# The Fourier part of a hybrid block on sums and differences of tokens and channels

## The chip, the cores and the metric

The kernel runs on one core of one Trainium2 chip. The metric is the device time in microseconds of one execution, and of several the median. A core has a matmul engine (PE, with its weight loads listed as PEld), a vector engine (DVE), a scalar engine (ACT), a general engine (POOL, also called GpSimd) and a queue engine (SP), each of which works through its own list of instructions in order and waits at semaphores for the others. Sixteen DMA engines move data between the chip's main memory and the core's on-chip memory.

## The reference, cut to what matters

One layer over 512 latent tokens (and 256 context tokens, which only feed the attention states): normalisation with modulation, one input projection of width 4128, two kinds of mixing, an output projection with a gated residual, and then experts.

```python
p = modulate(rms_norm(x, norm1_g), shift1, scale1) @ w_in
q, k, v, g, z_f, z_b, u = split(p)        # u: 1024 columns, the Fourier part
# attention heads (GLA): 4 heads over q, k, v and the gates from z_f, z_b
# Fourier part: 8 groups of 128 channels
uf = u.reshape(512, 8, 128)
y = jnp.fft.fft2(uf, axes=(tokens, channels), norm='ortho').real
mixed = concatenate([y_gla, y.reshape(512, 1024)], -1) @ w_out
x = x + gate1 * mixed
h = modulate(rms_norm(x, norm2_g), shift2, scale2)
aff = softmax(h @ w_router)               # 16 experts
gate, idx = top_k(aff.T, 64)              # each expert takes 64 tokens
# SwiGLU experts on the taken tokens, gated, scattered back; a final norm
```

The six modulation vectors come from silu(c) @ w_ada. The real part of a two-dimensional transform of real numbers is cos·cos − sin·sin over tokens l and channels c. The cosine is the same at l and 512 − l, and the sine changes its sign there; for the channels the same holds at c and 128 − c. Tokens 0 and 256 and channels 0 and 64 have no partner.

## The kernel before

**Products in three passes.** Matmul operands of the large products are split in two parts, a rounded one (hi) and the rest (lo), and a product is three matmuls: hi·hi, hi·lo and lo·hi (L481 to L483 for the input products, L875 to L877 for the output). Each has a stationary operand of 128 x 128, which is a tile of 128 tokens, and a moving one of 128 x 512 weights.

**The weights.** `Stream` (L155) brings `w_in` and `w_out` in chunks of 512 KB (two k rows of 128 by 512 columns). `load` issues a chunk's DMA on ACT's queue (L168), at most two chunks ahead; `split` makes hi with an ACT copy (L175) and lo with a DVE subtraction (L176), and chunks are split two ahead of the products that take them.

**The stages.** The stages run one after the other on PE: K, V and Q products (V and Q by `tokens`, L472), the gates G in two column blocks, the Fourier input u in two column blocks, and the output products in four blocks of 512 columns (L862 to L895) with 16 k rows each, the first 8 from the attention heads, the last 8 from the Fourier part. Then come the routing (L903 to L953, with the top-64 by eight rounds of MAX8 and MATCH_REPLACE8 at L935 and L936) and the experts. The Fourier stage reads tokens by stride (`four`) and folds them in its `ev` into halves with two DVE operations per tile.

**Work in the background.** `bg` is a planner: generators put their instructions between the products, and each `yield` says after how many microseconds of estimated PE time the next step stands (`bg.tick`). So the order of the program is set by estimates, and every engine then runs its list in that order. In the background run: the later modulation vectors (`ada_rest`, L416, 16 steps of one load of 1 MB on SP and one DVE operation at L430, the delay of a step is `RD[0]` or `RD[1]`), the attention heads (`gla_head`, L537) with the transposes of their gated output (`gla`, L678), the Fourier transforms (`fourier`, L698), and the routing logits of the output (`logits`, L850). Two vectors, i = 2 and 4, run in V and Q (`rest1`), i = 3 and 5 in the output products (`rest_out`, L760).

**Space.** All large tiles are pages of 128 x 2048 from a pool of 24 (`PG`); the expert weights are loaded ahead into pages as these come free (`pump`, L829, on SP's queue). Eight PSUM banks hold results.

## Time and profile before

| what | value |
|---|---|
| time, median of 3 runs | 1827.98 us (1825.45 to 1828.62) |
| the profiled execution | 1827.28 us, its span 1825.2 us |
| PE busy | 1728.1 us, 95% of the span |
| DVE busy | 689.0 us, 38% |
| ACT busy | 336.8 us, 18% |
| POOL busy | 5.5 us, 11 instructions |
| moved by DMA | 571.79 MB, mean 313 GB/s |

The stretches of the span are: V and Q products 161.3 to 339.4 us, gates 339.4 to 405 and 405 to 472, Fourier input 472 to 613.4, output products 613.4 to 821.5 (the transforms of the second half of the channels lie in the first 32.6 us), routing 821.5 to 845.3, and experts after it. A fast matmul is listed with 0.39 us, because matmuls overlap; what one costs is the distance from one start to the next. A matmul in full 32-bit precision has two rows in the trace.

### The profile page before, as it was taken

The numbers are of one execution on the slowest core, as the hardware profiler recorded it, in microseconds if no ns is written. First come the engines' busy times: TensorE is split into PE (matmuls) and PEld (weight loads), VectorE is DVE, ScalarE is ACT, GpSimd is POOL, SyncE is SP. The second block draws the span as 40 slices with busy tenths as digits, with TensorE's granted clock in tenths as the row PEclk, the third lists the DMA queues.
The fourth block names the chain that finished last, engine by engine and source line by source line (L and its number), as shares of the span: only waits on it lengthen the run. The fifth ranks groups of instructions, "written<-read, shape, count | busy, mean of one in ns | idle before, by whom it ended". The sixth has DMA issues, their size and how long they took to land.

```text
span 1825.2 us, 21307 instructions
## 1 busy us (share of the span) xinstructions
PE 1728.1 (95%) x8992; PEld 1049.1 (57%) x8992; DVE 689.0 (38%) x1072; ACT 336.8 (18%) x564; POOL 5.5 (0%) x11
## 2 busy tenths in 40 slices
...
GB/s 375 391 230 180 261 211 340 84 70 81 58 81 178 287 263 275 292 174 331 379 300 319 419 419 419 419 420 419 420 419 419 420 419 419 420 419 410 415 419 254
DMA packets 89695, 571.79 MB, mean 313 GB/s; under 512 B 9840, under 2 KB 12312, under 8 KB 27136
## 3 DMA queue, kind: packets, MB, share of 16 engines
...
q14 instruction: 25, 0.20, 0.0%
HBM read 566.21 MB, written 4.19 MB: 313 GB/s over the span
## 4 chain that ended last, share of the span: by engine, by line
PE 77%; DMA 15%; DVE 4%; ACT 3%; issue 1%; DVEq 0%; ACTq 0%; SPq 0%
PE bank L1072 18%; PE bank L1131 10%; DMA pg<-in_w_e_gate 7%; PE bank L991 6%; PE bank L481 5%; PE bank L482 5%; PE bank L483 5%; DMA pg<-in_w_e_up 4%; PE bank L875 3%; DMA pg<-in_w_e_down 3%; PE bank L877 3%; PE bank L876 3%; PE bank L1034 3%; PE bank L331 2%; PE bank L332 2%; PE bank L333 2%
## 5 line engine op out<-in xcount | busy, mean ns | idle before, releaser
L1072 PE MATMUL bank<-pg,pg 128*64 128x512 f32 x1856 | 435.2, 597 | 25.7 <-DMA pg<-in_w_e_up 13.9
L1072 PEld LDWEIGHTS bank<-pg,pg 128*64 128x64 f32 x1856 | 139.1, 136 | 287.9 <-issue 219.4
L1131 PE MATMUL bank<-pg,tp 128*64 128x512 f32 (+1 forms) x1056 | 233.4, 584 | 11.3 <-ACT tp L1099 10.8
L481 PE MATMUL bank<-pg,pg 128*128 128x512 f32 x448 | 184.5, 412 | 1.5 <-ACT pg L175 1.4
L482 PE MATMUL bank<-pg,pg 128*128 128x512 f32 x448 | 175.5, 392 | 0.8 <-DVE pg L176 0.8
L483 PE MATMUL bank<-pg,pg 128*128 128x512 f32 x448 | 175.5, 392 | 0.0
L176 DVE TENSOR_TENSOR pg<-pg,pg 128x1024 fp32r<-128x1024 f32 x96 | 117.4, 1223 | 130.9 <-ACT pg L175 120.8
L1131 PEld LDWEIGHTS bank<-pg,tp 128*64 128x64 f32 x1056 | 74.7, 137 | 145.3 <-issue 123.2
L995 DVE TENSOR_SCALAR pg<-bank,a,b 128x128 f32<-128x128 f32 x116 | 41.4, 406 | 302.6 <-PE bank L991 302.6
L430 DVE SCALAR_TENSOR_TENSOR pg<-pg,scol,pg 128x2048 f32<-128x2048 f32 x60 | 140.9, 2348 | 27.0 <-DMA pg<-in_w_ada 26.8
L175 ACT ACTIVATE pg<-pg 128x1024 fp32r<-128x1024 f32 x96 | 101.7, 1059 | 204.7 <-DVE pg L430 61.7
L1037 DVE TENSOR_TENSOR pg<-pg,bank 128x512 f32<-128x512 f32 (+1 forms) x132 | 79.7, 666 | 152.5 <-PE bank L1034 152.5
L991 PEld LDWEIGHTS bank<-pg,pg 128*128 128x128 f32 x896 | 104.0, 192 | 32.1 <-issue 28.4
L991 PE MATMUL bank<-pg,pg 128*128 128x128 f32 x896 | 111.5, 280 | 0.0
L875 PE MATMUL bank<-pg,pg 128*128 128x512 f32 x256 | 105.1, 410 | 0.0
L877 PE MATMUL bank<-pg,pg 128*128 128x512 f32 x256 | 100.1, 391 | 0.0
L876 PE MATMUL bank<-pg,pg 128*128 128x512 f32 x256 | 100.0, 391 | 0.0
L481 PEld LDWEIGHTS bank<-pg,pg 128*128 128x128 f32 x448 | 85.3, 190 | 21.5 <-ACT pg L175 1.9
L482 PEld LDWEIGHTS bank<-pg,pg 128*128 128x128 f32 x448 | 85.3, 190 | 17.7 <-DVE pg L176 1.1
L483 PEld LDWEIGHTS bank<-pg,pg 128*128 128x128 f32 x448 | 85.0, 190 | 17.8
L1106 ACT ACTIVATE tp<-bank 128x512 f32<-128x512 f32 x16 | 9.4, 597 | 431.4 <-PE bank L1072 431.4
L331 PE MATMUL bank<-pg,pg 128*128 128x512 f32 x192 | 72.3, 377 | 0.8 <-ACT pg L321 0.8
(256 smaller groups left out, 1611.7 us busy)
## 6 DMA issues: line engine op xcount, KB each, us to landing
pg<-in_w_e_gate SPq DMA_DIRECT2D x128, 1024.0 KB, 19.9
pg<-in_w_e_up SPq DMA_DIRECT2D x128, 1024.0 KB, 19.9
...
```

What stands on the lines that cost most here:

```text
L176: dve.tensor_sub(p[:, 1024:].bitcast(F32R), src, p[:, :1024])
L331: pe.matmul(o, w[0], h[0], start=first, stop=False, skip_group_check=sgc)
L430: dve.scalar_tensor_tensor(acc, p, scol[:, k:k + 1], acc, op0=OP.mult, op1=OP.add)
L481: pe.matmul(bs[t], h[0], whi[:, kk, :], start=k == 0, stop=False)
L482: pe.matmul(bs[t], h[0], wlo[:, kk, :], start=False, stop=False)
L483: pe.matmul(bs[t], h[1], whi[:, kk, :], start=False, stop=k == 15)
L875: pe.matmul(bs[t], h[0], whi[:, kk, :], start=k == 0, stop=False)
L876: pe.matmul(bs[t], h[0], wlo[:, kk, :], start=False, stop=False)
L877: pe.matmul(bs[t], h[1], whi[:, kk, :], start=False, stop=k == 15)
L991: pe.matmul(b[:, j * 128:(j + 1) * 128], X[t][:, k * 128:(k + 1) * 128], ohr[:, t, :], start=t == 0, stop=t == 3)
L1072: pe.matmul(gu[2 * m + f][64 * j:64 * j + 64, :], xe(pr, k)[:, 64 * j:64 * j + 64], v3(ps[2 * m + j], 2)[:, k2, f * 512:f * 512 + 512], st ...
L1131: pe.matmul(b[64 * j:64 * j + 64, :h.stop - h.start], hidt[:, 4 * f + k, 64 * j:64 * j + 64], v3(ps[j], 4)[:, k, h], start=f == 0 and k == ...
```

## The change

**Input products of the Fourier part.** They run on folded operands. The normalised tokens `hl` are folded while the second gate block runs (`fold_h`): POOL adds hi and lo, DVE makes the sums l + (512 − l) and the differences, which are split into hi and lo again in place. The host lays the columns of `w_in` out so that channels c and 128 − c stand in the two halves of a chunk, and `Stream.fold` makes their sum (DVE) and difference (POOL) before the split. One pass over 16 chunks then does what two column blocks did: sums of tokens meet sums of channels, differences meet differences. Token 256 is a product of one row; channel 64 comes with the gates' small product (`w_z` widened by 8 columns).

**Transforms.** They run on halves: 257 tokens with cosines, 255 with sines, and 64 channels of two groups together. Channel 64 of all groups goes by 8-row products.

**Output products.** The last 4 chunks of each column block of `w_out` are folded in the same manner (16 chunks of 32). The part of the result that is even in the output token is accumulated in banks 0 and 1 and the odd part in banks 2 and 3. The gated output of the heads is folded as well after its transposes. Two tiles (t, t + 2) are then combined to their sum and difference. The order of the tokens within the kernel is 0 to 256 and 511 down to 257: `x` is loaded in that order and the host puts the output back. The top-64 works on scores put back to the order of the tokens.

**Modulation.** Vector 3 moves from `rest_out` into `rest1`, and `RD[0]` falls from 5.0 to 3.4.

```diff
-RD = (5.0, 4.6)
+RD = (3.4, 4.6)
...
-            if self.nl < len(self.chunks) and self.nl < self.ns + 2:
+            if self.nl < len(self.chunks) and self.nl < (max(self.ns, self.nf) if self.ns in self.folded else self.ns) + 2:
...
+        def fold(self, j):
+            if j in self.folded and self.nf <= j:
+                while self.nl <= j:
+                    self.load()
+                r, f = self.raw(j), self.fw[j % 2]
+                dve.tensor_add(f[:, :512], r[:, :512], r[:, 512:])
+                pool.tensor_sub(f[:, 512:], r[:, :512], r[:, 512:])
+                self.nf = j + 1
         def split(self):
+            n = self.ns
             self.load()
-            src = self.raw(self.ns)
+            self.fold(n)
+            if self.ahead and n + 1 in self.folded:
+                self.load()
+                self.fold(n + 1)
+                self.load()
+            src = self.fw[n % 2] if n in self.folded else self.raw(n)
             p = PG.get()
             act.activation(p[:, :1024].bitcast(F32R), src, AF.Copy)
             dve.tensor_sub(p[:, 1024:].bitcast(F32R), src, p[:, :1024])
...
-    rest1 = rest((2, RD[0]), (4, RD[0]))
+    rest1 = rest((2, RD[0]), (4, RD[0]), (3, RD[0]))
...
-            act.activation(yt(m, 0), b, AF.Copy, scale=gng[:, m:m + 1])
-            dve.scalar_tensor_tensor(yt(m, 1), b, gng[:, m:m + 1], yt(m, 0).bitcast(F32),
-                                     op0=OP.mult, op1=OP.subtract)
+            y, z = tmp(), tmp()
+            act.activation(y, b, AF.Copy, scale=gngh[:, m:m + 1])
             BK.put(b)
+            dve.tensor_add(z[:, 0:1], y[:, 0:1], y[:, 256:257])
+            dve.tensor_sub(z[:, 256:257], y[:, 256:257], y[:, 0:1])
+            dve.tensor_add(z[:, 1:256], y[:, 1:256], y[:, 511:256:-1])
+            dve.tensor_sub(z[:, 257:512], y[:, 511:256:-1], y[:, 1:256])
+            act.activation(yt(m, 0), z, AF.Copy)
+            dve.tensor_sub(yt(m, 1), z, yt(m, 0).bitcast(F32))
...
+        def tokens_dft(p):
+            ps = slice(128 * p, 128 * p + 128)
+            vf, b = vfs[p % 2], BK.get()
+            d = DY[:, 260 + p:261 + p]
+            for i, (st, tb) in enumerate(((uv[:, 0, ps], CT[:, 0, :]), (uv[:, 1, ps], CT[:, 1, :]), (uv[0:1, 2, ps], row))):
+                pe.matmul(b[:, 0:256], st, tb[:, 0:256], start=i == 0, stop=i == 2, skip_group_check=True)
+                pe.matmul(d, st, tb[:, 256:257], start=p == 0 and i == 0, stop=i == 2, skip_group_check=True)
+            for i in range(2):
+                pe.matmul(b[:, 256:512], uv[:, 2 + i, ps], ST[:, i, :], start=i == 0, stop=i == 1, skip_group_check=True)
+            (dve.tensor_copy if p % 2 else act.copy)(vf[:, 0:512], b)
+            dve.tensor_copy(vf[:, 512:513], d)
...
-        yield from rest((3, RD[1]))
+        bg.drain(rest1)
...
+    def fold_h():
+        FF.append(PG.get())
+        ws.fw = [FF[0][:, 1024:2048], FF[0][:, 0:1024]]
+        x, y = FF[0][:, 0:512], FF[0][:, 512:1024]
+        pool.memset(y[:, 256:257], 0.0)
+        for k in range(NK):
+            while kdone[0] <= k:
+                yield 1.3
+            hi, lo = hl(k, 0), hl(k, 1)
+            if k % 4 == 0:
+                for s in range(2):
+                    act.copy(h256[:, k:k + 4, s], v3(HL[k // 4][s], 4)[:, :, 256].bitcast(F32R))
+            pool.tensor_add(x[:, 0:512], hi.bitcast(F32), lo.bitcast(F32))
+            act.copy(y[:, 0:1], x[:, 0:1])
+            dve.tensor_add(y[:, 1:256], x[:, 1:256], x[:, 511:256:-1])
+            dve.tensor_sub(y[:, 257:512], x[:, 1:256], x[:, 511:256:-1])
+            act.activation(hi, y, AF.Copy)
+            dve.tensor_sub(lo, y, hi.bitcast(F32))
+            yield 2.2
...
-        tokens(48 + 8 * c, four, ev)
+    bg.drain(hfold)
+    ws.ahead = True
+    bs = [BK.get() for _ in range(4)]
+    for k in range(NK):
+        whi, wlo = ws.take(FW0 + k)
+        for t, f in enumerate(lat):
+            h = (f(k, 0), f(k, 1))
+            i = t // 2
+            pe.matmul(bs[t], h[0], whi[:, i, :], start=k == 0, stop=False, skip_group_check=True)
+            pe.matmul(bs[t], h[0], wlo[:, i, :], start=False, stop=False, skip_group_check=True)
+            pe.matmul(bs[t], h[1], whi[:, i, :], start=False, stop=k == 15, skip_group_check=True)
+            bg.tick(0.65)
+        for s, w in ((0, whi), (0, wlo), (1, whi)):
+            pe.matmul(bs[2][0:1, :], h256[:, k, s:s + 1], w[:, 0, :], start=False, stop=k == 15 and s == 1,
+                      skip_group_check=True)
+        bg.tick(0.5)
+        ws.done(FW0 + k)
...
-            for kk in range(2):
-                k = 2 * j + kk
-                h = [yt(k, s)[:, t * 128:(t + 1) * 128] for s in range(2)]
-                pe.matmul(bs[t], h[0], whi[:, kk, :], start=k == 0, stop=False)
-                pe.matmul(bs[t], h[0], wlo[:, kk, :], start=False, stop=False)
-                pe.matmul(bs[t], h[1], whi[:, kk, :], start=False, stop=k == 15)
-            bg.tick(1.3)
-            if j == 7:
-                s = tmp()
-                dve.tensor_mul(s, bs[t], g1[0][:, cs])
-                dve.tensor_add(X[t][:, cs], X[t][:, cs], s)
-                act.activation(s, X[t][:, cs], AF.Square, accum_out=ssx[:, t, c:c + 1])
-                bg.add(logits(c, t), LD[0])
+            i, ts = t // 2, slice(t * 128, (t + 1) * 128)
+            for k, q in ((2 * j, 0), (2 * j + 1, 1)) if j < 4 else ((4 + j, i),):
+                h = [yt(k, s)[:, ts] for s in range(2)]
+                pe.matmul(bs[t], h[0], whi[:, q, :], start=k == 0, stop=False, skip_group_check=True)
+                pe.matmul(bs[t], h[0], wlo[:, q, :], start=False, stop=False, skip_group_check=True)
+                pe.matmul(bs[t], h[1], whi[:, q, :], start=False, stop=k == 11 and t == 3, skip_group_check=True)
+            if t == 2 and j >= 4:
+                for s, w in ((0, whi), (0, wlo), (1, whi)):
+                    pe.matmul(bs[2][0:1, :], dT[:, j - 4, s:s + 1], w[:, 0, :], start=False, stop=False,
+                              skip_group_check=True)
+            if t < 3 and j == 7:
+                y = Y64[0][0:72, ts if t < 2 else slice(256, 257)].bitcast(F32R)
+                pe.matmul(bs[t][0:128 if t < 2 else 1, :], y, W64[0][0:72, cs].bitcast(F32R), start=False, stop=True,
+                          skip_group_check=True)
+            bg.tick(1.3 if j < 4 else 0.75)
+            if j == 7 and t >= 2:
+                t0 = t - 2
+                ps, qs = tmp(), tmp()
+                dve.tensor_mul(ps, bs[t0], g1[0][:, cs])
+                dve.tensor_mul(qs, bs[t], g1[0][:, cs])
+                for x, f in ((X[t0][:, cs], dve.tensor_sub), (X[t][:, cs], dve.tensor_add)):
+                    dve.tensor_add(x, x, ps)
+                    f(x, x, qs)
+                for r in (t0, t):
+                    act.activation(ps if r == t0 else qs, X[r][:, cs], AF.Square, accum_out=ssx[:, r, c:c + 1])
+                    bg.add(logits(c, r), LD[0])
...
+    dve.tensor_copy(aft[:, 0:257], b[:16, 0:257])
+    dve.tensor_copy(aft[:, 257:512], b[:16, 511:256:-1])
...
+    for v in (work, sl):
+        dve.tensor_copy(aft[:, 0:255], v[:, 511:256:-1])
+        dve.tensor_copy(v[:, 257:512], aft[:, 0:255])
```

How the program's order moves is shown for three places. In these rows `pg_76_1343` is a page by its numbers, then come the operands and the size.

DVE in the V products, of the kernel before: L430 is a step of the modulation vector, L176 the split of a weight chunk.

```order
L430 SCALAR_TENSOR_TENSOR pg_76_1343<-pg_86_1497,scol,pg_76_1343 128x2048
L176 TENSOR_TENSOR pg_88_1528<-pg_6_99,pg_88_1528 128x1024
L430 SCALAR_TENSOR_TENSOR pg_76_1343<-pg_87_1524,scol,pg_76_1343 128x2048
L176 TENSOR_TENSOR pg_90_1571<-pg_6_99,pg_90_1571 128x1024
L430 SCALAR_TENSOR_TENSOR pg_76_1343<-pg_89_1549,scol,pg_76_1343 128x2048
L430 SCALAR_TENSOR_TENSOR pg_76_1343<-pg_91_1580,scol,pg_76_1343 128x2048
L176 TENSOR_TENSOR pg_93_1617<-pg_6_99,pg_93_1617 128x1024
L430 SCALAR_TENSOR_TENSOR pg_76_1343<-pg_92_1607,scol,pg_76_1343 128x2048
```

One or two steps stand between two splits there. The same place of the changed kernel, where the step is L472 and the split L204:

```order
L204 TENSOR_TENSOR pg_84_1457<-pg_6_103,pg_84_1457 128x1024
L472 SCALAR_TENSOR_TENSOR pg_76_1353<-pg_83_1447,scol,pg_76_1353 128x2048
L472 SCALAR_TENSOR_TENSOR pg_76_1353<-pg_85_1472,scol,pg_76_1353 128x2048
L204 TENSOR_TENSOR pg_87_1503<-pg_6_103,pg_87_1503 128x1024
L472 SCALAR_TENSOR_TENSOR pg_76_1353<-pg_86_1487,scol,pg_76_1353 128x2048
L472 SCALAR_TENSOR_TENSOR pg_76_1353<-pg_88_1512,scol,pg_76_1353 128x2048
L472 SCALAR_TENSOR_TENSOR pg_76_1353<-pg_89_1527,scol,pg_76_1353 128x2048
L204 TENSOR_TENSOR pg_91_1552<-pg_6_103,pg_91_1552 128x1024
```

Between two splits it is now mostly two steps, up to three.

DVE in the second gate block, of the kernel before: the decays of an attention head (L551 to L589) and one split (L176).

```order
L551 SCALAR_TENSOR_TENSOR pg_159_3068<-bank_107_3086,pg_159_3068 128x512
L552 SCALAR_TENSOR_TENSOR pg_159_3068<-bank_108_3087,pg_159_3068 128x256
L554 SCALAR_TENSOR_TENSOR pg_159_3068<-pg_72_1249,pg_159_3068 128x768
L176 TENSOR_TENSOR pg_160_3110<-pg_6_99,pg_160_3110 128x1024
L572 TENSOR_TENSOR pg_158_3067<-pg_158_3067 128x512
L573 TENSOR_SCALAR pg_158_3067<-pg_158_3067 128x256
L585 TENSOR_TENSOR st<-st 128x4
L586 TENSOR_TENSOR pg_158_3067<-pg_158_3067,pg_119_2089 128x512
L587 TENSOR_TENSOR pg_158_3067<-pg_158_3067,pg_72_1249 128x256
```

There the head and the split have DVE to themselves. The same place of the changed kernel: L594 to L631 are the head's, L204 is the split, L884, L885 and L887 belong to the fold of the tokens, and `pg_168_2855` is its working page.

```order
L597 SCALAR_TENSOR_TENSOR pg_177_3197<-pg_72_1256,pg_177_3197 128x768
L884 TENSOR_TENSOR pg_168_2855<-pg_168_2855 128x255
L885 TENSOR_TENSOR pg_168_2855<-pg_168_2855 128x255
L887 TENSOR_TENSOR pg_50_814<-pg_168_2855,pg_49_813 128x512
L204 TENSOR_TENSOR pg_178_3253<-pg_6_103,pg_178_3253 128x1024
L615 TENSOR_TENSOR pg_176_3196<-pg_176_3196 128x512
L616 TENSOR_SCALAR pg_176_3196<-pg_176_3196 128x256
L628 TENSOR_TENSOR st<-st 128x4
L629 TENSOR_TENSOR pg_176_3196<-pg_176_3196,pg_129_2144 128x512
L630 TENSOR_TENSOR pg_176_3196<-pg_176_3196,pg_72_1256 128x256
L631 TENSOR_TENSOR pg_176_3196<-pg_176_3196,pg_71_1255 128x512
```

A chunk's sum, difference and low part are put between the head's operations, and all of them wait in one list.

ACT around the start of the Fourier input, of the kernel before, with what each waits for: L168 loads a chunk, L175 makes its high part.

```order
L460 COPY pg_184_3807<-bank_156_3862 128x512 [waits PE_49]
L168 DMA pg_6_99<-in_w_in 128x1024 [waits DVE_49]
L175 ACTIVATE pg_188_3873<-pg_6_99 128x1024 [waits DMAHW2_49]
L168 DMA pg_6_99<-in_w_in 128x1024 [waits DVE_49]
L175 ACTIVATE pg_192_3908<-pg_6_99 128x1024 [waits DMAHW3_49]
L717 COPY pg_190_3884<-bank_157_3919 128x512 [waits PE_49]
```

Each load waits for DVE alone and has its high part right behind it. The same of the changed kernel: L180 loads, L203 makes the high part of a folded chunk, L886 that of a folded token row block, L668 is a head's.

```order
L883 COPY pg_168_2855<-pg_168_2855 128x1 [waits DVE_49,Pool_49]
L886 ACTIVATE pg_63_1043<-pg_168_2855 128x512 [waits DVE_49,Activation_49]
L180 DMA pg_6_103<-in_w_in 128x1024 [waits DMAHW3_49]
L180 DMA pg_6_103<-in_w_in 128x1024 [waits DMAHW4_49,DVE_49,Pool_49]
L180 DMA pg_6_103<-in_w_in 128x1024 [waits DMAHW5_49,DVE_49,Pool_49]
L203 ACTIVATE pg_183_3454<-pg_168_2855 128x1024
L668 COPY pg_180_3263<-bank_120_3463 128x256 [waits PE_49]
L669 COPY pg_180_3263<-bank_120_3463 128x256
```

A load now waits for DVE and POOL, which fold the chunk in the buffer that it overwrites, and stands ahead of the next high part in ACT's list.

## Rows read from the trace of the kernel before

**Rows 1.** The page: span, engines (busy, share, instructions), chain that ended last by engine.

```profile
span 1825.2 us, 21307 instructions
...
PE 1728.1 (95%) x8992; PEld 1049.1 (57%) x8992; DVE 689.0 (38%) x1072; ACT 336.8 (18%) x564; POOL 5.5 (0%) x11
...
PE 77%; DMA 15%; DVE 4%; ACT 3%; issue 1%; DVEq 0%; ACTq 0%; SPq 0%
```

**Rows 2.** Busy time by stretch: us, PE, PEld, DVE, ACT, POOL, PEclk, DMA share, GB/s.

```profile
161.30:250.00 88.70, 88.70 (x391) 72.58 (x390) 53.81 (x34) 17.41 (x20) 0.00 (x0) 1.00 0.66 243
250.00:339.40 89.40, 89.40 (x402) 73.24 (x401) 53.60 (x33) 17.75 (x20) 0.95 (x1) 1.00 0.73 265
339.40:405.00 65.60, 63.20 (x345) 51.34 (x344) 29.14 (x44) 31.39 (x54) 0.95 (x1) 1.00 0.22 71
405.00:472.00 67.00, 61.37 (x350) 49.61 (x348) 42.86 (x72) 33.89 (x64) 0.95 (x1) 0.97 0.20 66
472.00:613.40 141.40, 136.36 (x699) 112.12 (x700) 85.56 (x124) 59.60 (x105) 0.95 (x1) 1.00 0.37 127
...
646.00:821.50 175.50, 175.38 (x891) 138.33 (x893) 99.77 (x86) 48.49 (x76) 0.00 (x0) 1.00 0.68 252
821.50:845.30 23.80, 16.58 (x73) 8.16 (x70) 17.15 (x41) 2.55 (x7) 0.00 (x0) 0.86 1.00 415
850.00:1000.00 150.00, 148.65 (x816) 73.84 (x814) 37.69 (x104) 9.56 (x15) 0.00 (x0) 1.00 0.83 324
1000.00:1750.00 750.00, 718.88 (x3512) 314.74 (x3510) 147.91 (x307) 34.72 (x58) 0.00 (x0) 1.00 1.01 419
```

**Rows 3.** PE in order of time, end of the Q products: start us, us, engine, line, operation.

```profile
329.89 0.39 PE L331 MATMUL bank<-pg,pg 128*128 128x512 f32 x1
...
331.93 0.39 PE L331 MATMUL bank<-pg,pg 128*128 128x512 f32 x1
```

**Rows 4.** Chain that ended last, pieces in order of time: start us, us, what.

```profile
573.52 1.73 PE bank L715 x8
...
578.03 0.86 PE bank L722 x2
...
678.14 0.79 PE bank L441 x8
```

**Rows 5.** Instructions of DVE by line and form: count, busy us, mean ns, idle before.

```profile
L430 DVE SCALAR_TENSOR_TENSOR pg<-pg,scol,pg 128x2048 f32<-128x2048 f32 x60 | 140.9, 2348 | 27.0 <-DMA pg<-in_w_ada 26.8
L176 DVE TENSOR_TENSOR pg<-pg,pg 128x1024 fp32r<-128x1024 f32 x96 | 117.4, 1223 | 130.9 <-ACT pg L175 120.8 <-PE bank L544 9.2 <-DMA pg<-in_w_ada 0.8
...
L882 DVE TENSOR_TENSOR pg<-pg,tp 128x512 f32<-128x512 f32 x16 | 11.1, 692 | 0.5
...
L587 DVE TENSOR_TENSOR pg<-pg,pg 128x256 f32<-128x256 f32 x8 | 3.4, 422 | 1.0 <-ACT pg L575 1.0
```

**Rows 6.** DVE in order of time, V and Q products: start us, us, idle before.

```profile
178.27 2.35 DVE L430 SCALAR_TENSOR_TENSOR pg<-pg,scol,pg 128x2048 f32<-128x2048 f32 x1 [2.14 <-DMA pg<-in_w_ada]
...
198.88 2.35 DVE L430 SCALAR_TENSOR_TENSOR pg<-pg,scol,pg 128x2048 f32<-128x2048 f32 x1
...
261.32 1.29 DVE L428 TENSOR_SCALAR pg<-pg,scol 128x2048 f32<-128x2048 f32 x1 [4.66 <-DMA pg<-in_w_ada]
265.17 2.35 DVE L430 SCALAR_TENSOR_TENSOR pg<-pg,scol,pg 128x2048 f32<-128x2048 f32 x1 [2.56 <-DMA pg<-in_w_ada]
...
293.04 2.35 DVE L430 SCALAR_TENSOR_TENSOR pg<-pg,scol,pg 128x2048 f32<-128x2048 f32 x1 [1.14 <-DMA pg<-in_w_ada]
```

**Rows 7.** Waits of SP's queue from 161.3 to 339.4: us in total, times, longest.

```profile
SPq L424 <- PE bank L483: 56.6, 10, 14.4
```

**Rows 8.** Instructions of POOL by line and form, as rows 5.

```profile
L598 POOL MEMSET pg<- 128x1024 f32 x4 | 3.8, 953 | 379.9 <-DVE pg L430 212.0 <-PE bank L483 167.9
...
L151 POOL MEMSET spad<- 128x512 f32 x1 | 0.5, 524 | 0.3 <-POOLq L1239 0.3
```

**Rows 9.** SP in order of time, first of the expert weights.

```profile
745.92 7.36 SPq L838 DMA_DIRECT2D pg<-in_w_e_gate  x2
```

265 lines of the change are left out of this document (170 added, 95 removed).

## The prediction

> **What bounds the kernel now.** I read the page's totals first, and the reader should see that PE is busy 95% of the span and holds 77% of the chain that ended last, DMA 15%, DVE 4% [rows 1]. A mean over stages decides nothing, so the table by stretch comes next [rows 2]. From 161.3 to 339.4 us (V and Q products) PE never idles. The two gate stretches and the Fourier input stretch (339.4 to 613.4) hold 2.4, 5.6 and 5.0 us of idle PE, 13.0 in all. In the output products (646 to 821.5) it is full, in the routing (821.5 to 845.3) it waits and the DMA share is 1.00. From 850 to 1000 PE is busy 148.65 of 150 at a DMA share of 0.83, from 1000 on the weight stream is full (1.01, 419 GB/s). So until 1000 a PE microsecond taken away is worth one, unless something late takes its place; what the experts do afterwards follows at a fixed distance, if their weights are issued earlier too.
>
> The work goes against the profiled execution, 1827.3 us (span 1825.2), 0.7 under the median of the three runs, 1827.98; at that distance the forecast compares with either.
>
> **Products.** Ten matmul starts from 329.89 to 331.93 us are nine intervals of 0.227 us for 128x128 by 128x512 [rows 3]. The input products of the Fourier part fall from 2 column blocks x 16 chunks x 4 tiles x 3 = 384 to 16 x (4 x 3 + 3) = 240, the last 3 one-row ones for token 256, which still stream 512 columns. That is -144 x 0.227 = -32.6 us. The output products fall from 4 x 64 x 3 = 768 to 4 x (96 + 60 + 3) = 636: -132 x 0.227 = -29.9 us.
>
> **Transforms.** Now there are 32 matmuls of 256 columns, eight trace rows (four matmuls) of which take 1.73 us, and 16 of 512 columns at 0.86 for two rows (one matmul) [rows 4]: 13.8 + 13.8 = 27.6 us. After there are 40 of about 256 columns, 40 x 0.43 = 17.3, and 25 of one column; eight rows of the ada sum, whose columns are few as well, took 0.79, so 0.20 each, 5.0 [rows 4]. Together -5.3 us.
>
> **End of the output products.** The pair (t, t+2) is combined by six DVE operations after the last matmul, not two after each tile. Four more of 0.69 (L881 and L882 take that) lie between PE's end and the routing [rows 5], +2.8. In the routing two copies of the 16x512 scores and four of 16x255 stand in the top-k chain; at the 0.42 of a 256-column DVE operation (L587) they are 6 x 0.4 = +2.4 [rows 5]. Nothing covers these: +5.2.
>
> The sum without waits: -32.6 - 29.9 - 5.3 + 5.2 = -62.6 us.
>
> **Waits in V and Q.** The third modulation vector (i=3) moves there out of the output products, and the step delay falls from 5.0 to 3.4. Forty-eight steps and three starts are then to be done in 178.1 us, 3.6 to 3.7 us a step. A step is one DVE operation of 2.35 us (L430), a split 1.22 (L176) [rows 5], with one split in two to three steps: DVE's load allows it. The pace of today is another matter. Five steps from 178.27 to 198.88 took 4.12 each, six from 265.17 to 293.04 took 4.65, and at the start of a vector DVE idled 4.66, each time until the w_ada chunk came in [rows 6]. Yet those loads were themselves held: SP waited 56.6 us in ten waits on PE to free a page [rows 7], which a shorter delay relieves. Behind a late step stand the splits on DVE, and behind them PE. At 4.12 the work is 48 x 4.12 + 14 = 212 against 178: 34 us late; at 3.6 nothing. I take +7, near the lower end, as the waits on PE make most of today's pace; range 0 to 34.
>
> **Waits in gates and Fourier input.** The fold of the normalised tokens puts 16 x (0.42 + 0.42 + 0.69) = 24.5 us on DVE (prices of L587 and L882, [rows 5]) into a stretch of 67.0 where it is busy 42.9 [rows 2]: 67.4, full. In the Fourier stretch the folded weights need 16 x (0.69 + 1.22) = 30.6, the GLA heads left over 25 (1.4 of 29.1 - 9 x 1.22 = 18.1, one head's in the stretch from 339.4 to 405 [rows 2]), the transposes of their output 8 x 1.84 = 14.7 (0.42 + 0.42 + 0.69 and 0.3 for two one-column ones): 71. PE has some 86 to do there: 240 x 0.227 = 54.4, 28 for the heads (1.4 of 63.2 - 8 x 24 x 0.227 = 19.7), 3.6 more. So there is cover, yet it is thin, and single buffers make a chain: POOL adds, ACT copies a column, DVE adds and subtracts, ACT rounds, DVE subtracts, and POOL may begin the next. On ACT the load of a coming chunk now waits for DVE and POOL to have folded the one before, with the copy that PE needs queued behind it. I take once more the 13.0 us that PE idles there now; between 0 and 30, which is 16 chunks late by the difference of two DVE steps, 1.9.
>
> **Waits in the output products.** Each column block folds four chunks (4 x 1.91), with 4 splits at 1.22, 12 operations of 0.69 and eight ada steps of 2.35: 40 us on DVE, and on PE 159 x 0.227 + 3 = 39. There is no ada vector 3 there any more, and chunks are held two ahead. I take +4, range 0 to 10.
>
> **The POOL operations.** POOL does 5.5 us now, memsets alone [rows 1]; after, it gets 16 adds and 32 subtractions of 512 columns. No row shows POOL reading two tiles. The near ones are its memsets, 0.95 for 1024 columns, 0.52 for 512 [rows 8]; half of the first (0.48) from below, DVE's 1.22 for twice the columns (L176) from above. I take 0.95. At that, 16 x 0.95 = 15 us lie beside 67, and nothing is late by the rate alone. The Trainium skill, GPSIMD Engine Reference, section "Elementwise — side-by-side cycle accounting", has a measured 4497 ns for an fp32 add of 2048 elements; by that an estimate for 512 is 1.1 us, the sum stays what it is, and the 46 us of case C below would be 53. No row here shows it.
>
> All in all -62.6 + 7 + 13 + 4 = -38.6: 1788.7, so 1789 us.
>
> **Rivals.**
> - Case A (0.52): the forecast, 1789, with a range of its own of 1777 to 1803.
> - Case B (0.20): the waits stay under 10 us since every unit has room and the slack of a prepared chunk (8 us in V, 5 in Q) (36 or 24 matmuls of 0.227) swallows a late step: 1827.3 - 62.6 + 3 = 1768. For it: PE idles 13 in 340 now. Against it: DVE is planned full in two stretches.
> - Case C (0.18): POOL and DVE don't run side by side. Then the 48 POOL operations of 0.95, 46 us in all, count on DVE as well, where it is full: in the second gate stretch 15, in the Fourier stretch 15, in the output 15. PE is late by all of the first, where DVE has no room, and by a third of the other 31, where it has some: 26, so 1789 + 26 = 1815. Nothing in the trace speaks for or against, since POOL's few memsets never stood beside a long DVE stretch. A rule of the Trainium skill (SBUF — State Buffer, section "Who interferes with whom") says that GpSimd shares a port pair with VectorE and the lock on it is exclusive, so that a VectorE instruction with two inputs in SBUF blocks, or is blocked by, a GpSimd one that reads SBUF. No run here shows it yet, and by it this case would come.
> - Case D (0.07), slower: the w_ada ring in V and Q keeps its pace of 4.65 [rows 6] and PE waits for it. 48 x 4.65 + 3 x 4.7 = 237 us against 178, +59, with the other 17 of waits: 1827.3 - 62.6 + 59 + 17 = 1841. It decides from about 4.37 us a step, where 48 steps and starts eat 46 us. For it: the pace is seen. Against: the loads' waits on PE are what the delay sets, and the DMA share in those stretches is 0.66 and 0.73 [rows 2].
> - Case E (0.03): the work is shortened but the end is set by the weight stream, which starts no earlier: 1827. Against: its first loads are issued at 745.92 in SP's row [rows 9], in the program's order as pages come free, so it moves with the products; and from 850 to 1000 PE still paces.
>
> **How the numbers follow.** The likeliest is A, 1789. D, E, a part of C (what lies above 1815, 0.05) and of B (below 1764, 0.05) are 0.20 together: the range is 1764 to 1815. Faster by over 0.2% (3.7 us, what a measurement of this kernel can tell from none): A, B and C, 0.90; within 0.2%: E, 0.03; slower: D, 0.07.
>
> **What would show it.** Right: the Fourier input stretch is 141.4 - 38 or so, 613.4 to 821.5 shorter by some 30; V and Q within 10 us of 178; the end of the routing some 38 us earlier and the experts unchanged from there. Wrong: PE waiting on DVE's split (the rounded weights) in V and Q with DVE waiting on w_ada (D); DVE's operations, 0.42, 0.69 and 1.22, getting longer wherever POOL is busy, or the POOL operations above 1.2 (C); experts that start earlier and end with the same time (E). If PE's waits are as now in the gates and under 3 us elsewhere, B. A start interval other than 0.227 in the new products, for the one-row ones above all, would upset the first term itself.

## The result, and the profile after

The changed kernel takes 1893.27 us (median of 4 runs, 1891.63 to 1899.28), the kernel before 1828.3 in the same comparison: the ratio is 1.0361, interval 1.0332 to 1.0389. It is slower by 65 us; the forecast was 1789, faster, with a range of 1764 to 1815. The profiled execution has a span of 1891.0 us.

The page of the changed kernel: span, engines with busy time, share and instructions, and the chain that ended last by engine.

```profile
span 1891.0 us, 21143 instructions
...
PE 1702.4 (90%) x8756; PEld 1011.0 (53%) x8756; DVE 761.1 (40%) x1188; ACT 343.3 (18%) x593; POOL 82.9 (4%) x61
...
PE 38%; DMA 18%; DVE 6%; ACT 2%; issue 1%; POOL 0%; ACTq 0%; DVEq 0%; SPq 0%; POOLq 0%
```

Against [rows 1] PE has 26 us less busy time in a span 66 us longer, and its share of the chain that ended last falls from 77% to 38%: this program is no longer one in which PE sets the pace until the experts. POOL has 82.9 us where 5.5 were.

The same view by stretch as [rows 2], with the changed kernel's own limits: V and Q products, the two gate blocks, the time until the Fourier input begins, the Fourier input, the output products, routing, experts. Columns are us, PE, PEld, DVE, ACT, POOL, PEclk, DMA share, GB/s.

```profile
161.50:352.80 191.30, 186.39 (x815) 150.88 (x814) 137.13 (x86) 36.17 (x42) 0.00 (x0) 0.97 0.83 316
352.80:430.00 77.20, 67.60 (x351) 54.18 (x351) 39.23 (x51) 34.30 (x58) 2.42 (x3) 0.93 0.25 82
430.00:507.20 77.20, 62.12 (x340) 50.02 (x339) 58.49 (x92) 36.05 (x82) 16.62 (x13) 0.89 0.13 41
507.20:526.00 18.80, 3.78 (x40) 2.71 (x39) 12.39 (x21) 8.84 (x20) 4.68 (x4) 0.64 0.10 29
526.00:657.20 131.20, 100.51 (x457) 73.65 (x456) 79.33 (x139) 51.59 (x89) 25.74 (x18) 0.87 0.35 121
657.20:880.40 223.20, 198.08 (x954) 149.63 (x952) 128.74 (x131) 57.11 (x88) 31.76 (x16) 0.95 0.49 175
880.40:911.10 30.70, 19.91 (x85) 10.07 (x84) 20.75 (x50) 3.74 (x10) 0.00 (x0) 0.78 0.97 406
911.10:1891.00 979.90, 922.32 (x4592) 414.21 (x4592) 217.22 (x472) 64.72 (x129) 0.00 (x0) 0.99 0.96 395
```

The experts take 979.9 us as before (1825.2 - 845.3). All that changed lies ahead of them, and in every stretch PE now idles and the granted clock is under 1.00. Between gates and Fourier input stand 18.8 us in which PE is busy for 3.8.

The lengths of the stages (in us, from the starts of the products' lines in the profiled executions). V and Q end with the last Q product and the gates with the last gate product; "until F" goes from there to the first product of the Fourier input (474.7 in the kernel before, 2.7 behind the limit that [rows 2] have), and "after" from the last output product to the end. The medians are those of the timed runs; a profiled execution can differ from the median of its kernel by up to 9.5 us (e5).

| kernel | V and Q | gates | until F | Fourier input | output | after | median |
|---|---|---|---|---|---|---|---|
| before | 177.7 | 131.0 | 4.6 | 138.9 | 207.4 | 1004.2 | 1828 |
| changed | 190.5 | 154.6 | 18.8 | 131.4 | 222.7 | 1010.9 | 1893 |
| e1 fold after split | 187.2 | 154.2 | 17.5 | 129.8 | 212.6 | 1011.0 | 1880 |
| e2 no POOL | 192.5 | 158.4 | 18.3 | 132.7 | 218.7 | 1012.2 | 1894 |
| e3 vector back | 182.1 | 146.5 | 18.5 | 131.8 | 265.8 | 1012.2 | 1920 |
| e4 no token fold | 185.7 | 141.4 | 8.6 | 124.7 | 222.2 | 1010.7 | 1857 |
| e5 no weight fold | 195.2 | 153.1 | 15.9 | 113.6 | 218.4 | 1011.5 | 1861 |
| e6 lazy token fold | 192.0 | 154.4 | 18.6 | 132.6 | 219.9 | 1010.4 | 1895 |
| e7 one pass in F | 188.2 | 154.7 | 18.8 | 126.2 | 224.8 | 1010.3 | 1891 |
| e8 e1 and e6 | 195.8 | 155.5 | 19.8 | 124.1 | 211.6 | 1011.1 | 1876 |
| e9 no folds | 189.9 | 139.0 | 4.7 | 104.7 | 212.0 | 1011.4 | 1827 |
| e10 three heads | 188.3 | 154.8 | 18.7 | 124.4 | 202.2 | 1011.0 | 1861 |
| e11 no vector 3 | 190.5 | 148.1 | 18.9 | 131.1 | 219.6 | 1010.8 | 1885 |
| e12 no folds, no vector 3 | 191.3 | 132.4 | 5.3 | 105.4 | 213.3 | 1010.8 | 1824 |
| e13 logits later | 193.9 | 155.4 | 18.7 | 131.5 | 224.3 | 1012.1 | 1896 |
| e14 no vector 3, delay 5 | 180.7 | 146.4 | 18.6 | 131.7 | 222.9 | 1010.7 | 1874 |
| e15 token fold staged | 192.8 | 145.5 | 13.7 | 132.9 | 223.2 | 1011.4 | 1882 |
| e16 three orders | 196.1 | 148.2 | 12.3 | 130.5 | 208.6 | 1012.1 | 1869 |
| e17 before, vector 3 moved | 188.9 | 139.0 | 4.6 | 139.7 | 205.0 | 1004.4 | 1842 |
| e18 three orders, delay 4.2 | 184.5 | 147.3 | 13.6 | 130.1 | 211.1 | 1012.6 | 1861 |

V and Q lie between 185.7 and 196.1 us in kernels that are alike there (e4 and e16 are the ends), so differences of less than 10 us in that column mean nothing by themselves.

### The profile page after: what moved, and what is told of

The parts are those of the page before. It is cut to its first block, busy times and chain, and to the rows that moved or that the text cites. A ratio compares the mean times of both kernels' runs of the same rounds, so it can differ in the third digit from the quotient of the medians.

```text
span 1891.0 us, 21143 instructions
## 1 busy us (share of the span) xinstructions
PE 1702.4 (90%) x8756; PEld 1011.0 (53%) x8756; DVE 761.1 (40%) x1188; ACT 343.3 (18%) x593; POOL 82.9 (4%) x61
## 4 chain that ended last, share of the span: by engine, by line
PE 38%; DMA 18%; DVE 6%; ACT 2%; issue 1%; POOL 0%; ACTq 0%; DVEq 0%; SPq 0%; POOLq 0%
PE bank L1222 16%; DMA pg<-in_w_e_up 10%; PE bank L1281 9%; PE bank L1141 5%; DMA pg<-in_w_e_down 4%; PE bank L1184 2%; DMA pg<-in_w_e_gate 2%; DMA pg<-in_w_out 2%; DVE pg L204 1%; ACT pg L203 1%; PE bank L1006 1%; PE bank L1007 1%; PE bank L1005 1%; DVE pg L472 1%; PE bank L501 0%
## 5 line engine op out<-in xcount | busy, mean ns | idle before, releaser
L204 DVE TENSOR_TENSOR pg<-pg,pg 128x1024 fp32r<-128x1024 f32 x96 | 122.5, 1280 | 109.5 <-ACT pg L203 95.2
L1281 PEld LDWEIGHTS bank<-pg,tp 128*64 128x64 f32 x1056 | 74.5, 137 | 145.8 <-issue 124.1
L472 DVE SCALAR_TENSOR_TENSOR pg<-pg,scol,pg 128x2048 f32<-128x2048 f32 x60 | 140.9, 2349 | 27.1 <-DMA pg<-in_w_ada 26.6
L203 ACT ACTIVATE pg<-pg 128x1024 fp32r<-128x1024 f32 x96 | 100.9, 1058 | 268.7 <-DVE pg L472 79.3
L523 PE MATMUL bank<-pg,pg 128*128 128x512 f32 x320 | 131.8, 412 | 13.6 <-ACT pg L203 13.6
L524 PE MATMUL bank<-pg,pg 128*128 128x512 f32 x320 | 128.8, 402 | 2.2 <-DVE pg L204 2.2
L525 PE MATMUL bank<-pg,pg 128*128 128x512 f32 x320 | 128.1, 400 | 0.0
L1141 PEld LDWEIGHTS bank<-pg,pg 128*128 128x128 f32 x896 | 104.0, 192 | 32.1 <-issue 29.2
L1005 PE MATMUL bank<-pg,pg 128*128 128x512 f32 x192 | 80.3, 418 | 5.5 <-ACT pg L203 5.5
L1006 PE MATMUL bank<-pg,pg 128*128 128x512 f32 x192 | 78.5, 409 | 5.7 <-DVE pg L204 5.7
L523 PEld LDWEIGHTS bank<-pg,pg 128*128 128x128 f32 x320 | 62.3, 195 | 30.4 <-ACT pg L203 14.9
L1007 PE MATMUL bank<-pg,pg 128*128 128x512 f32 x192 | 77.1, 402 | 0.0
L1285 DVE SCALAR_TENSOR_TENSOR pg<-bank,gcol,pg 128x512 f32<-128x512 f32 (+1 forms) x33 | 24.2, 735 | 125.1 <-PE bank L1281 125.0
L360 PE MATMUL bank<-pg,pg 128*128 128x512 f32 x192 | 71.8, 374 | 0.9 <-ACT pg L350 0.8
L524 PEld LDWEIGHTS bank<-pg,pg 128*128 128x128 f32 x320 | 62.4, 195 | 15.8 <-DVE pg L204 3.3
```

What stands on the lines that cost most here:

```text
L203: act.activation(p[:, :1024].bitcast(F32R), src, AF.Copy)
L204: dve.tensor_sub(p[:, 1024:].bitcast(F32R), src, p[:, :1024])
L472: dve.scalar_tensor_tensor(acc, p, scol[:, k:k + 1], acc, op0=OP.mult, op1=OP.add)
L523: pe.matmul(bs[t], h[0], whi[:, kk, :], start=k == 0, stop=False)
L524: pe.matmul(bs[t], h[0], wlo[:, kk, :], start=False, stop=False)
L525: pe.matmul(bs[t], h[1], whi[:, kk, :], start=False, stop=k == 15)
```

## The experiments

Theory L was: each fold costs by its place in the in-order lists of ACT and DVE. Its rivals were P (POOL is slow and holds up DVE), R (the third vector makes V and Q late), B (the attention heads' chain is what sets the shorter stages) and, later, S (the step delay, not the number of steps) and Q (the logits of a pair). Line numbers in the rows of an experiment are its own.

**Which folds cost what: e4, e5, e9.** e4 has the first of these edits, e5 the other two, e9 all:

```diff
-            pool.tensor_add(x[:, 0:512], hi.bitcast(F32), lo.bitcast(F32))
-            act.copy(y[:, 0:1], x[:, 0:1])
-            dve.tensor_add(y[:, 1:256], x[:, 1:256], x[:, 511:256:-1])
-            dve.tensor_sub(y[:, 257:512], x[:, 1:256], x[:, 511:256:-1])
-            act.activation(hi, y, AF.Copy)
-            dve.tensor_sub(lo, y, hi.bitcast(F32))
...
-                dve.tensor_add(f[:, :512], r[:, :512], r[:, 512:])
-                pool.tensor_sub(f[:, 512:], r[:, :512], r[:, 512:])
...
-            src = self.fw[n % 2] if n in self.folded else self.raw(n)
+            src = self.raw(n)
```

> Leaves out the fold of the normalised tokens (POOL add, two DVE operations, two roundings and a column copy for each of 16 rows); the Fourier input products take the tokens unfolded. Theory L: the gate stretches and the 18.8 us between them and the Fourier input lose the waits behind the fold (3.4 + 6.5 + 3.5 + 11.5 us on the heads' transposes) and their low clock; 30 to 40 us less, 1853 to 1863. Theory P: only the lengthened L887 (16 x 0.5 us) and POOL's 16 adds go from DVE and POOL, at most 10 us less, 1883 to 1890. Theory R: no change.

> Leaves out the folds of the 32 weight chunks (DVE's add and POOL's subtraction); the products take the chunks unfolded. Theory L (the folds stand in the lists ahead of what PE needs): the Fourier input loses its waits on L203 and L204 (some 22 us) and most of its low clock, the output products some 15 us as well; 35 to 50 less than 1893, 1843 to 1858. Theory B (background): with 240 products for 384 the Fourier input is shorter than the chain of the attention heads that runs beside it on ACT, DVE and PE in turn, and that chain sets its length; then the Fourier input stays within 10 us of 131 and only the output gains, 1870 to 1885.

> Leaves out both the folds of the tokens and those of the weight chunks; their two runs alone took 37 and 32 us off 1893. Theory L (each fold costs by its own place in the lists): the two add, 1820 to 1830. Theory B (the heads' chain, closer to the products' end than before, sets what is left): the second gain finds less, the Fourier input with the gap before it stays above 110 us and the whole is 1835 to 1850.

e4 measured 1857 (ratio to before 1.0159, interval 1.0134 to 1.0185), e5 1861 (1.0183, 1.0151 to 1.0216), e9 1827 (1.0003, 0.9986 to 1.0020). The two add up as L said: 37 + 32 = 69, and 66 were measured. But e5 missed both of its ranges, L's by 3.5 us: in its profiled execution, which took 1871 and is the longest of its four, the Fourier input is shorter by 18 us and the output only by 4, where L wanted 22 and 15. And e9 says more than was asked: with the folds of tokens and of weights free of charge the shorter products are worth nothing yet, since the kernel is then at the time of the one before. (The third fold, that of the heads' gated output, and the combination of the output tiles stay in e9; what the third fold costs was not tried.)

**Order or work: e1, e6, e8, e15, e16.** e1 moves four lines of `split` behind its two operations; e6 replaces the drain by a step for each row (with one buffer for folded weights till the fold is through); e8 is e1 and e6; e15 spreads a row of the token fold over four steps of the planner; e16 is e1, e13 and e15. The first two pieces below are e1's, the next two e6's, the last is part of e15's.

```diff
-            if self.ahead and n + 1 in self.folded:
...
             self.ns += 1
+            if self.ahead and n + 1 in self.folded:
...
-    bg.drain(hfold)
...
+        while hdone[0] < min(k + 3, NK):
+            bg.step(next(e for e in bg.gens if e[1] is hfold))
...
+        for s in range(NK + 3):
+            if s >= 3:
+                dve.tensor_sub(hl(s - 3, 1), ys[(s - 3) % 2], hl(s - 3, 0).bitcast(F32))
+            if 2 <= s < NK + 2:
+                act.activation(hl(s - 2, 0), ys[s % 2], AF.Copy)
```

> The fold of chunk n+1 and its loads are put behind the split of chunk n, not ahead of it; nothing else differs from the changed kernel (1893 us). Theory L (lists): PE waits because fold steps stand ahead of what it needs in ACT's and DVE's lists; in the Fourier input, L203 stands behind a load that waits for the next chunk's fold, ten waits of 2 to 3 us there and five in the output products. The swap takes away most of them and of the low clock behind them: 15 to 25 us less in the Fourier input, 5 to 10 in the output, 1860 to 1873 in all. Theory P (POOL): its operations are slow (1.28 and 1.73 us) and lengthen DVE's beside them; they stay, so the time stays within 5 us of 1893. Theory R (ring): the third vector's steps in V and Q make everything late; no change either.

> The token folds that are left at the end of the gates are no longer all issued before the Fourier input; each is issued two rows ahead of the product that takes it, and until the last of them the folded weights have one buffer instead of two. Theory L: the 18.8 us between gates and Fourier input, in which PE runs 40 small matmuls, shrink to under 8, as the evacuation that PE waits for (11.5 us) no longer stands behind five folds in ACT's list; 1875 to 1883 if the rest of the Fourier input stays at 131. Theory B: the head's chain goes on at its own pace, what the gap loses the Fourier input gains, 1888 to 1898.

> The two orders together: token folds issued as they are needed, and the fold of the next chunk behind the split of the one before. Theory L: the gains add, 13 from the first order as measured and 10 to 18 from the other: 1862 to 1872. Theory B: 1878 to 1885.

> The token fold does the same operations on the same engines, with each row's four stages spread over four steps of the planner, so that no engine's list has a stage right behind the one it waits for. Theory L: most of the 37 us of the token fold are waits within lists, and go: 15 to 30 us less, 1863 to 1878. If the fold costs by its work (DVE's 24 us, POOL beside it), it stays within 6 us of 1893.

> Three changes of order alone, with all the work of the changed kernel: the next chunk's fold behind the split, the logits of a pair later, the token fold in stages. Theory L: the gains add, 13 + 8 to 15 + 15 to 30: 1835 to 1857. If the work itself is the bound, 1870 to 1880.

e1: 1880 (1.0277, 1.0250 to 1.0304), a smaller gain than L promised, and the 10 us came from the output, not from the Fourier input. e6: 1895, no change, and the 18.8 us stayed. But e6 does not test what it was made for. Of the five roundings that start after 510 us in the changed kernel, three stand ahead of the evacuation that PE waits for, and in e6 the same three still do (its ACT starts them at 511.92, 517.57 and 521.45). The last of them, the evacuation (L649) and PE's wait in e6:

```profile
521.45 0.63 ACT L888 ACTIVATE pg<-pg 128x512 fp32r<-128x512 f32 x1 [1.75 <-DVE pg L887]
521.98 0.84 ACT L649 COPY pg<-bank 128x256 f32<-128x256 f32 x2
```

```profile
522.39 1.11 PE L648 MATMUL bank<-cst,pg 128*128 128x128 f32 x4 [12.58 <-ACT pg L649]
```

Only the two folds behind it came later. So e6 speaks neither for nor against L; e4, in which the token fold is gone, has 8.6 us at this place, and the kernel before 4.6. e8: 1876, the first order alone; it missed both of its ranges. e15: 1882 (1.0293, 1.0278 to 1.0308): 11 us for the same work in another order, where 15 to 30 were expected, all from the gates and the time until F. e16: 1869 (1.0217, 1.0198 to 1.0236), 24 in all, where L wanted 36 to 58. So about 24 us are order; the rest of the folds' 66 did not go by any order that was tried. In e16 the Fourier input and the output read (columns as above):

```profile
517.00:647.50 130.50, 100.93 (x460) 74.26 (x457) 79.55 (x144) 52.39 (x92) 27.06 (x17) 0.86 0.34 122
647.50:856.10 208.60, 194.15 (x948) 146.35 (x947) 124.83 (x131) 56.59 (x87) 25.38 (x16) 0.97 0.52 188
```

The output is down to 208.6 us with 14.5 idle, the Fourier input has still a granted clock of 0.86 and 29.6 idle.

**POOL: e2.** DVE does what POOL did:

```diff
-                pool.tensor_sub(f[:, 512:], r[:, :512], r[:, 512:])
+                dve.tensor_sub(f[:, 512:], r[:, :512], r[:, 512:])
...
-            pool.tensor_add(x[:, 0:512], hi.bitcast(F32), lo.bitcast(F32))
+            dve.tensor_add(x[:, 0:512], hi.bitcast(F32), lo.bitcast(F32))
```

> The 16 adds and 32 subtractions of POOL are done by DVE. Theory P: DVE's operations go back to their lengths (1.20 to 0.69 for the low part of the tokens) and the chains lose 0.6 to 1.0 us at each POOL step; 20 to 35 us less, 1858 to 1873. Theory L: DVE's list, in which the folds stand among the heads' operations, gets 48 x 0.69 = 33 us more work; the waits shift but don't go, 1885 to 1905. Theory R: no change.

1894 (1.0346, 1.0312 to 1.0381): no change, as L said. What P says of the durations is true all the same. POOL's operations in the changed kernel (count, busy, mean ns, idle before):

```profile
L190 POOL TENSOR_TENSOR pg<-pg 128x512 f32<-128x512 f32 x32 | 55.3, 1727 | 262.6 <-DMA pg<-in_w_out 157.5 <-DVE pg L204 97.7 <-DMA pg<-in_w_in 4.5
L882 POOL TENSOR_TENSOR pg<-pg,pg 128x512 f32<-128x512 f32 x16 | 20.5, 1280 | 94.1 <-DVE pg L885 81.8 <-ACT pg L883 12.3
```

DVE's beside them:

```profile
L204 DVE TENSOR_TENSOR pg<-pg,pg 128x1024 fp32r<-128x1024 f32 x96 | 122.5, 1280 | 109.5 <-ACT pg L203 95.2 <-PE bank L587 9.3 <-issue 4.8
...
L189 DVE TENSOR_TENSOR pg<-pg 128x512 f32<-128x512 f32 x32 | 27.3, 853 | 27.0 <-DMA pg<-in_w_out 25.6 <-DMA pg<-in_w_in 1.3
...
L887 DVE TENSOR_TENSOR pg<-pg,pg 128x512 fp32r<-128x512 f32 x16 | 18.7, 1171 | 15.9 <-ACT pg L886 15.9
```

and the same three lines in e2, where POOL has none:

```profile
L204 DVE TENSOR_TENSOR pg<-pg,pg 128x1024 fp32r<-128x1024 f32 x96 | 117.1, 1223 | 103.0 <-ACT pg L203 92.8 <-PE bank L587 9.4 <-DMA pg<-in_w_ada 0.7
...
L189 DVE TENSOR_TENSOR pg<-pg 128x512 f32<-128x512 f32 x32 | 22.0, 687 | 24.8 <-DMA pg<-in_w_out 24.1 <-DMA pg<-in_w_in 0.6
...
L887 DVE TENSOR_TENSOR pg<-pg,pg 128x512 fp32r<-128x512 f32 x16 | 11.1, 692 | 14.8 <-ACT pg L886 14.8
```

The low part of the tokens goes from 1171 back to 692 ns, the sum of the weights from 853 to 687, the split from 1280 to 1223. That is 16 x 0.48 + 32 x 0.17 + 96 x 0.06 = 19 us of DVE that POOL's 48 operations cost it. In e2 DVE does those 48 itself at 0.68, 33 us. One loss stands against the other, and the time is the same. What POOL's part costs by itself, without that work put on another engine, no run shows.

**PE or the lists: e7, e10.** e7 has the first edit (and the like for token 256), e10 the second:

```diff
-            pe.matmul(bs[t], h[0], whi[:, i, :], start=k == 0, stop=False, skip_group_check=True)
-            pe.matmul(bs[t], h[0], wlo[:, i, :], start=False, stop=False, skip_group_check=True)
-            pe.matmul(bs[t], h[1], whi[:, i, :], start=False, stop=k == 15, skip_group_check=True)
+            pe.matmul(bs[t], h[0], whi[:, i, :], start=k == 0, stop=k == 15, skip_group_check=True)
...
-        for n in range(NH):
+        for n in range(NH - 1):
```

> Leaves out two of the three passes of the Fourier input products, 160 of 240 matmuls, 36 us of PE at full clock; all folds, splits and heads stay. If PE (at its low clock) sets the length of the Fourier input, it falls by 36 us or more: 1850 to 1857. Theories L and B: other engines' lists set it, it stays within 10 us of 131, 1883 to 1897.

> Leaves out the fourth attention head, 20 us of PE, 18 of DVE and its ACT work, nearly all of it in the Fourier input; all folds stay. Theory B: the head's chain of operations in turn on ACT, DVE and PE sets the Fourier input, which falls from 131 to under 100 us; 1850 to 1862 in all. Theory L: the folds of the chunks, two or three waits per chunk, set it, and it falls by no more than 15; 1875 to 1885.

e7: 1891. The Fourier input of e7:

```profile
521.00:647.20 126.20, 69.68 (x298) 51.15 (x297) 80.45 (x139) 51.03 (x89) 25.61 (x18) 0.72 0.35 126
```

PE is busy 69.7 of 126.2 us, with two thirds of the products gone, and the stage is 5 us shorter than with all of them. PE does not set it, and its granted clock of 0.87 in the changed kernel is for the most part a symptom there, not a cost. e10: 1861, the time that B gave, but not in B's place: the Fourier input lost 7 us (L's "no more than 15"), the output 20. This does not refute B, as the work behind the head moves up with it. The steps of vector 5 (L472) all lie in the output of the changed kernel; in e10 five of them lie in the Fourier input:

```profile
L472 DVE SCALAR_TENSOR_TENSOR pg<-pg,scol,pg x15: 2340/2346/2352, 664.8 to 793.5; 128x2048 f32<-128x2048 f32 x15
```

```profile
L472 DVE SCALAR_TENSOR_TENSOR pg<-pg,scol,pg x5: 2339/2344/2346, 607.6 to 642.6; 128x2048 f32<-128x2048 f32 x5
```

PE also waits 16.2 us in e10's Fourier input for a broadcast that follows the heads (L501), 3.8 in the changed kernel. So a head less makes the two stages shorter by 27 us together, and e10 does not tell L from B.

**The modulation vector: e3, e11, e14, e12, e17, e18.** e3 puts vector 3 back with the delay 5.0; e11 leaves it out; e14 is e11 with the delay 5.0; e12 is e9 and e11; e17 does the modulation part alone on the kernel before; e18 is e16 with 4.2.

```diff
-RD = (5.0, 4.6)
+RD = (3.4, 4.6)
...
-    rest1 = rest((2, RD[0]), (4, RD[0]))
+    rest1 = rest((2, RD[0]), (4, RD[0]), (3, RD[0]))
...
-        yield from rest((3, RD[1]))
+        bg.drain(rest1)
```

That is e17's edit. In the others `RD` and the two other lines are set accordingly; where vector 3 is left out, `dve.tensor_copy(b2, bsh2)` stands for it.

> Modulation vector 3 goes back from V and Q to the output products, with the step delay 5.0 as in the kernel before; the folds stay. Theory R: V and Q go from 191.3 back to 178 to 180 us and the first gate block loses its wait of 8.3 us and its low clock, 20 to 28 us less there, of which the output products take back 0 to 10: 1868 to 1880. Theories L and P: V and Q fall all the same by the few us of idle PE that stand there (4.9) and its low clock (5.7), the folds' waits from the second gate block on stay as they are, 1880 or a little above.

> Leaves out the third modulation vector altogether (its 16 loads, 16 steps and sums; the bias alone stands for it); the step delay stays 3.4. Theory R: V and Q go back to 178 to 181, the wait of 8.3 us at the first gate block goes and with it low clock there; 1893 becomes 1865 to 1873. Theories L and B: the vector costs what its idle time in V and Q shows, 5 us and as much for the clock; 1880 to 1886.

> As the run without vector 3 (1885 us, V and Q 190.5), with the step delay of the other two vectors back at 5.0. Theory S (step delay): the split of a weight chunk gets the page that a step has just read; steps that follow each other closer than their loads come in hold the split, so V and Q go back to 178 to 183 with the delay, 1872 to 1879. Theory W (work): V and Q are longer by the small products of channel 64 and the fold beside them, and stay at 188 to 192; 1885.

> Leaves out both folds and the third vector: what is left is the shorter products and transforms with the work that the kernel before had beside them, less one vector. If the waits come from folds and vector alone, this is near the sum without waits, 1827 - 63 = 1765, with a few us: 1765 to 1785. Theory B: the heads, transposes and the last vector find less room beside shorter products, and part of the gain stays away: 1790 to 1815.

> The kernel before with one part of the change alone: vector 3 in V and Q, step delay 3.4. Theory S (step delay and page): V and Q grow from 178 to 188 or more and the first gate block by some 5 us; the output products were full of PE work, so they give nothing back: 1840 to 1850. Rival: without folds the splits keep up, and the vector's steps hide as before: 1824 to 1832.

> The three orders together (1869 us) with a step delay of 4.2 in place of 3.4. Theory S: V and Q lose 5 to 10 us (from 196), the gates gain 2 to 5 by the steps that are left over for them; 1860 to 1867. Rival: what V and Q lose the gates gain, 1867 to 1873.

e3 went the other way: 1920 (1.0497, 1.0475 to 1.0519). V and Q fell to 182.1, yet the output grew to 265.8, and PE's longest wait in it is one of 35.2 us (us in total, times, longest), behind twelve steps in a row (start, us):

```profile
PE bank L478 <- DVE pg L472: 35.2, 1, 35.2
```

```profile
830.98 28.61 DVE L472 SCALAR_TENSOR_TENSOR pg<-pg,scol,pg 128x2048 f32<-128x2048 f32 x12
```

The planner's estimates of the output products fell from 166 to 131 us (four column blocks of 32 steps of 1.3; now each has 16 of 1.3 and 16 of 0.75), and two vectors of 16 steps at 4.6 are 147: what is left over is drained at one place, without products beside it. So, with that place as it is, the vector had to leave the output because the output became shorter. e11: 1885, V and Q still 190.5: R fell. e14: 1874 with V and Q at 180.7: S holds, 11 us come from the delay alone (1885 to 1874, one line of difference). V and Q in e14, then in e12, which has as many steps at 3.4:

```profile
160.50:341.20 180.70, 178.53 (x796) 146.09 (x795) 108.20 (x71) 35.74 (x41) 0.96 (x1) 1.00 0.67 250
```

```profile
159.80:351.10 191.30, 185.04 (x811) 149.61 (x810) 109.42 (x73) 36.28 (x42) 0.95 (x1) 0.97 0.63 236
```

In the changed kernel one sees how. In order of time (start, us, engine, idle before):

```profile
292.89 2.35 DVE L472 SCALAR_TENSOR_TENSOR pg<-pg,scol,pg 128x2048 f32<-128x2048 f32 x1 [2.70 <-DMA pg<-in_w_ada]
...
295.28 1.06 ACT L203 ACTIVATE pg<-pg 128x1024 fp32r<-128x1024 f32 x1 [10.99 <-DVE pg L472]
...
296.39 0.50 PE L523 MATMUL bank<-pg,pg 128*128 128x512 f32 x1 [1.97 <-ACT pg L203]
```

The vector's step waits 2.70 us for its load; the split's ACT copy takes the page that this step has read and has waited 10.99 us for it; PE waits 1.97 behind that. e17: 1842.5 (1.0071, 1.0054 to 1.0088), 14 us for this part alone, with nothing folded: V and Q grow by 11 us and the gates by 8, and the output gives 2 back. e18: 1861 (1.0178, 1.0162 to 1.0193), 8 us better than e16, V and Q at 184.5: the fastest version with all the work that was found, and 33 us behind the kernel before. e12: 1824 (0.9988, 0.9975 to 1.0000), where 1765 to 1785 was to be expected if folds and vector were all, and 1790 to 1815 by B: it missed both.

**The output: e13.** The two logits of a pair come 2 and 5 us of the planner's time later.

```diff
-                    bg.add(logits(c, r), LD[0])
+                    bg.add(logits(c, r), LD[0] + (2.0 if r == t0 else 5.0))
```

> The logits of a pair of output tiles are put 2 and 5 us of the planner's time later, one behind the other; nothing else. Theory Q (the pair): PE's transposes of X stand in its list right behind the pair's six DVE operations and then behind each other's evacuation, seven waits of 0.9 to 2.5 us in the output products with low clock behind them; later placement takes 8 to 15 us from the output products: 1878 to 1885. If these waits are only a symptom of folds that are late, the time stays within 4 us of 1893.

1896: no gain, Q fell. PE's waits in the output of the changed kernel and of e13:

```profile
PE bank L980 <- ACT pg L985: 5.9, 3, 2.5
PE bank L1006 <- DVE pg L204: 5.7, 9, 0.8
PE bank L1005 <- ACT pg L203: 5.5, 3, 2.0
```

```profile
PE bank L1005 <- ACT pg L203: 9.4, 6, 2.3
PE bank L1006 <- DVE pg L204: 7.5, 10, 0.8
```

The waits left the transposes of the logits (L980) and went to the next chunk's split (L1005, L1006), which stands behind the pair's six DVE operations in the same way. It was the pair, not the logits: whatever follows it in PE's list waits. Nor are these waits a symptom of late folds: in e12, which has no fold of tokens or weights, the transposes of the logits (L972 there) still wait for the pair's products and sums (L1014, L1018) and for an evacuation that ACT has behind the pair's squares (L977), 13.2 us of the 19.3 that PE idles in its output:

```profile
PE bank L972 <- ACT pg L977: 6.2, 3, 2.8
PE bank L972 <- DVE tp L1014: 4.5, 2, 3.2
PE bank L972 <- DVE pg L1018: 2.5, 1, 2.5
```

## Why the prediction was wrong

**What held.** The products cost what they were forecast to. At full clock the new ones start every 0.227 us, the one-row ones too (three of them share a row of 0.85 to 0.86), and both counts (240 and 636) are those of the trace. The tail after the last output product took 6.8 us more, 5.2 were forecast. The experts follow at their distance, so case E was no case.

**What failed: "Waits", the terms +7, +13 and +4.** The sum without waits was -62.6, the span changed by +65.8, so the waits were 128 us and not 24. By stage: V and Q +12.8, where 7 stood. Gates and Fourier input went from 274.4 to 304.8, while 32.6 of products and 13.8 of transforms (half of 27.6, all of which now lie in the output) had left it: 76.8, where 13 stood. The output grew by 15.2, while -29.9 + 13.8 - 5.3 should have come to -21.4: 36.6, where 4 stood. In the output PE's idle time is 223.2 - 198.1 = 25.1, and the low clock is 0.05 x 223.2 = 11.2: together 36.3, nearly the whole of it.

**Why it failed.** The step "So there is cover, yet it is thin" added up DVE's operations, 67 of 67 us and 71 of 86, and took what fits for what is hidden; "I take once more the 13.0 us" followed from it. DVE is busy 58.5 of 77.2 and 79.3 of 131.2 us in those stretches, never full, and leaving the two folds out gave back 66 us (e9). What counts, at least for the 24 us that went by order alone (e16), is the chain: an instruction that PE needs stands in a list behind one that waits for another engine. Around the end of the gates ACT does this (idle before, and for what):

```profile
519.33 0.63 ACT L886 ACTIVATE pg<-pg 128x512 fp32r<-128x512 f32 x1 [1.76 <-DVE pg L885]
...
522.12 0.63 ACT L886 ACTIVATE pg<-pg 128x512 fp32r<-128x512 f32 x1 [0.68 <-DVE pg L885]
522.66 0.84 ACT L648 COPY pg<-bank 128x256 f32<-128x256 f32 x2
```

and PE, at the same time:

```profile
523.07 1.12 PE L647 MATMUL bank<-cst,pg 128*128 128x128 f32 x4 [11.50 <-ACT pg L648]
```

Each rounding of tokens (L886) waits for DVE, DVE's next step in turn waits for the rounding (0.78 us at 519.99), and the evacuation that PE needs (L648) stands behind them. (e15 shows that spreading this chain gives back 9 of the gates' us and 5 of the 18.8 behind them.) In the Fourier input the turn of a chunk goes through a head's operation:

```profile
567.57 0.49 PE L919 MATMUL bank<-pg,pg 128*128 128x512 f32 x1 [1.69 <-ACT pg L203]
...
571.21 1.76 DVE L597 TENSOR_TENSOR_SCAN pg<-pg,pg 128x768 f32<-128x768 f32 x1
...
572.88 0.67 DVE L189 TENSOR_TENSOR pg<-pg 128x512 f32<-128x512 f32 x1
573.62 0.33 ACTq L180 DMA_DIRECT2D pg<-in_w_in  x1
574.00 1.06 ACT L203 ACTIVATE pg<-pg 128x1024 fp32r<-128x1024 f32 x1 [3.89 <-DVE pg L189]
...
575.11 0.50 PE L919 MATMUL bank<-pg,pg 128*128 128x512 f32 x1 [2.74 <-ACT pg L203]
576.43 0.50 PE L920 MATMUL bank<-pg,pg 128*128 128x512 f32 x1 [0.81 <-DVE pg L204]
```

DVE adds the chunk (L189) behind the head's scan (L597); ACT's load, and its copy of the next chunk behind it, wait for that; PE waits 2.74 for ACT and 0.81 more for DVE's low part. A chunk has 15 matmuls of 0.227, 3.4 us; this turn took 575.11 - 567.57 = 7.5. It is late by 4.1, where the upper end of the prediction's range had 1.9 for a chunk. That the fold's place ahead of the copy makes this stage long is not shown, however. e1 puts the fold behind the copy, and the stage stays at 130 us with nearly the same waits for the split (us in total, times, longest; the changed kernel first, then e1, where ACT's copy is L199 and DVE's low part L200):

```profile
PE bank L919 <- ACT pg L203: 12.7, 7, 2.7
...
PE bank L920 <- DVE pg L204: 5.8, 7, 0.8
```

```profile
PE bank L919 <- ACT pg L199: 10.0, 4, 4.4
PE bank L920 <- DVE pg L200: 7.6, 6, 2.4
```

It falls to 114 us when the fold's work is left out (e5).

**The clock was no term at all.** [rows 2] show 0.97 to 1.00 in these stages and the prediction took 1.00 for granted. Just after the two waits of 2.74 and 0.81 the products run at the lower of the two levels, 1.2 GHz, 0.43 us apart:

```profile
577.63 0.63 PE L921 MATMUL bank<-pg,pg 128*128 128x512 f32 x1
578.06 0.63 PE L919 MATMUL bank<-pg,pg 128*128 128x512 f32 x1
```

Where PE sets the pace (V and Q, the output) this adds to the wait that caused it: 5.7 us in V and Q (0.03 x 191.3), 11.2 in the output. In the Fourier input it costs little, by e7: 160 products less made the stage 5 us shorter.

**The rivals.** Case C had a mechanism that is there, and its price is not shown. POOL's operations do make DVE's longer, by the durations of e2, and they took 1.28 and 1.73, above the 0.95 taken and above the upper bound of 1.22. That agrees with the rule of the Trainium skill (SBUF — State Buffer, section "Who interferes with whom"): a VectorE instruction with two inputs in SBUF contends with a GpSimd one that reads SBUF. But taking it away by giving the work to DVE (e2) changed the time by nothing. Case D had the sign right and its size wrong: V and Q lost 13, not 59 us, and what was slow was not the pace of 4.65 but the delay of 3.4, which makes splits wait for pages that steps still hold. The prediction had this the wrong way round: it took a shorter delay to relieve the loads ("which a shorter delay relieves"), and between e14 and e11 the shorter one cost 11 us.

**What stays open.** e12 has no fold of tokens or weights and no vector 3. Its profiled execution, the fastest of its ten, is still 56 us over the sum without waits (58 by the medians): 14 in V and Q (S; e14 gave 11 of it back in the changed kernel), 15 between the gates and the end of the Fourier input, 27 in the output and 1 or 2 in the tail, less 2 before V. Of the 27, 13 are waits behind the pair, which the change itself brought in and the term +4 counted only as DVE's work. For the rest, what runs in the background stands closer together than before; that this density is the cause is argued, not shown, and the fold of the heads' output was never left out. Of the 66 us of the two folds, 24 went by order; why the other 42 stay is open too.
